# Samples' attention: float32 products on four strips of 32 array columns in place of two-part products per sequence, and a scan in two halves

## The chip, the cores and the metric

One core of one Trainium2 chip runs the whole kernel. The metric is the device time of one execution in microseconds; the kernel before has a median of 1036.18 us over three runs (1036.05 to 1041.79).

## What is computed

One step of a decoder layer for 512 prompt tokens and for 32 sample tokens: 8 sequences with 4 new tokens each and 1024 past tokens in pages of 128. Two attention branches read the same normalised input; a gated merge, an output projection, a SwiGLU FFN and a last norm follow. Everything is float32. The change concerns the two branches of the samples alone. Branch b (stick-breaking, 8 heads of 64) and branch a (softmax over 256 chosen keys, 8 query heads on 2 key heads) are, cut to what matters:

```python
# branch b, per sequence: q_b (4, 8, 64), keys and values (1028, 8, 64)
z = einsum('bthd,bshd->bhts', q_b, k) * HEAD_DIM ** -0.5
log_beta = log_sigmoid(z)
log_rest = where(strict, log_beta - z, 0.0)
later = cumsum(log_rest, axis=3, reverse=True) - log_rest
a = where(strict, exp(log_beta + later), 0.0)
o = einsum('bhts,bshd->bthd', a, v)
# branch a, per sequence: keys and values (1028, 2, 64), sel = the 256 chosen by the indexer
s = einsum('btcgd,btncd->btcgn', qg, sel_k) * HEAD_DIM ** -0.5
o = einsum('btcgn,btncd->btcgd', softmax(s), sel_v)
```

## The kernel before

A float32 matrix product is made of three or two products of fp32r operands: each operand is split into a part `h` (a copy rounded to fp32r, on ScalarE) and a rest `l` (the difference, on VectorE or POOL). Weights are split in `Weights._split` (L109 to L122), tokens once.

After the indexer's part (up to about 165 us), three generators are merged by `beside` (L1384): `samples` (budget S_COST), `heads` (the prompt's two attentions, H_COST) and the dense chain of projections and branch products (D_COST, matmuls at L504). `beside` always advances the stream whose share of yielded cost is lowest, so the yields and the budgets set how the streams mix; the tile framework's scheduler then orders the instructions of each engine once, when the program is built. On the chip each engine works through its queue in that order. The steps of top-k for the samples run beside (L639).

`samples` runs `sb_sample` (branch b) and then `dsa_sample` (branch a).

Branch b goes through two halves g of four sequences each. `logits` walks over two pairs of sequences, over c (pairs of pages), over b (the sequence of the pair) and jj (two pairs of heads each). `keys` (L1026) loads two pages of keys by `page` (SP's queue; at most eight page loads are outstanding, KV_B = 6 buffers of 128 x 512), turns them on TensorE (L1036, four transposes into one bank of tag `ts`), copies the bank rounded to `kk` on ScalarE (L1040) and takes the rest on VectorE (L1041). `scores` (L1055) multiplies, with queries of hi and lo parts in 128 stationary columns, four times per (c, b, jj) at L1063: 256 columns of keys each, 288 where the new tokens' keys stand behind. `sum_parts` (L1010) adds the hi and lo rows (ScalarE copy, VectorE add). `weights` (L1086) makes two sigmoids, one reversed scan over all 1056 keys (VectorE) and a product, yields W_LAT, turns the weights (L1100, L1104) and splits them. `values` (L1112) loads the value pages of one sequence after the other, splits each (ScalarE L1124, VectorE or POOL L1125) and multiplies with 64 stationary columns and 512 moving (L1131, two per page; the new tokens' values `vnew` have 32 rows). `fold` (L1144) turns the outputs (L1147) and adds the parts.

Branch a has its rows gathered by POOL (`keys_values`). Per pair of sequences `keys` (L1173) turns (L1177), copies (L1181) and takes the rest (L1182); `products` (L1188) adds the mask as a product (L1191) and four products of the parts (L1194); the softmax follows; `values` turns the weights (L1237), splits values (L1225 ScalarE, L1226 POOL), multiplies (L1249) and folds by a product with `stacked` (L1260).

`ones` and `sq` at L1518 and L1519, behind the samples' part, are plain float32 products on the whole array, and so are those of L817 in the indexer's part; transposes are float32 too.

## Time and profile before

| | us |
|---|---|
| median of three runs | 1036.18 |
| the profiled execution, its own time | 1040.26 |
| its span, first to last instruction | 1038.4 |
| PE busy / DVE / ACT / POOL | 978.4 / 772.9 / 548.5 / 400.8 |

PE is TensorE's matmuls, PEld its weight loads, DVE VectorE, ACT ScalarE, POOL GpSimd, SP the engine that issues most DMAs. In a group's row stand the line and engine, the operation, the tile written and those read (out<-in), the array's rows*columns and the shape, the count, then busy us and mean ns of one, and behind the last bar the idle time just before and what ended it. A matmul's length includes its way through the array, so successive matmuls overlap and their starts tell more than their lengths. In a matmul's shape 128*64 means 128 rows and 64 stationary columns, 128x512 the 512 moving columns.

### The profile page before, as it was taken

What the parts mean: (1) busy time and instruction counts of PE and PEld (TensorE: products, weight loads), DVE (VectorE), ACT (ScalarE), POOL (GpSimd) and SP (SyncE); (2) the same over time, 40 slices, a digit from 0 to 9 for tenths busy, and PEclk for the clock granted to TensorE, in tenths of its full rate; (3) what the DMA queues carried; (4) which work ended last, traced back from release to release, by engine and by line L of the source; (5) the groups of instructions that cost most, each with busy time, mean ns of one, the idle gap of its engine ahead of it and who ended that gap; (6) DMA issues with size and microseconds to landing.
All of it is one profiled execution on the core that took longest, in us unless ns stands there. A gap on an engine that the chain in (4) does not pass through costs nothing.

```text
span 1038.4 us, 20529 instructions
## 1 busy us (share of the span) xinstructions
PE 978.4 (94%) x7374; PEld 925.7 (89%) x7374; DVE 772.9 (74%) x1521; ACT 548.5 (53%) x1089; POOL 400.8 (39%) x345
## 2 busy tenths in 40 slices
PE   5999999898899998999899999989999999999995
PEld 4999998787778998889689999989999999999995
DVE  4568996789887895777785766896787787875774
ACT  6224435466654655766687745543444445542453
POOL 4545545103762126462726844511233223200331
PEclk9999999899999999999899999999999999999998
DMA  9775646787886659854523873502433331234312
GB/s 276 184 201 165 165 125 200 250 225 211 233 251 204 203 168 286 244 195 144 180 80 130 281 207 103 143 21 82 120 96 91 102 100 49 65 89 138 107 46 87
DMA packets 184703, 162.13 MB, mean 156 GB/s; under 512 B 13338, under 2 KB 148058, under 8 KB 183578
## 3 DMA queue, kind: packets, MB, share of 16 engines
q1 hardware_dynamic: 179434, 145.85, 48.4%
q0 software_dynamic: 1872, 10.75, 3.0%
q10 hardware_dynamic: 3296, 4.23, 1.4%
q8 instruction: 58, 0.95, 0.4%
q14 instruction: 43, 0.35, 0.1%
HBM read 133.37 MB, written 22.01 MB: 150 GB/s over the span
## 4 chain that ended last, share of the span: by engine, by line
PE 69%; DVE 11%; DMA 8%; issue 5%; ACT 2%; POOL 2%; SPq 2%; ACTq 1%; DVEq 0%; POOLq 0%
PE mm L504 14%; PE ffB L1630 8%; PE ffC L1630 5%; PE ffA L1630 5%; PE acc L504 5%; PE acc L1131 3%; PE acc L1715 3%; PE z L504 2%; PE ts L1036 2%; PE acc L1063 2%; PE dnB L1808 2%; POOL wl L119 2%; PE tp L865 2%; PE tp L878 2%; DMA kb<-in_cache_kv_b 1%
## 5 line engine op out<-in xcount | busy, mean ns | idle before, releaser
L119 POOL TENSOR_TENSOR wl<-wst,wh 128x512 fp32r<-128x512 f32 (+2 forms) x136 | 167.4, 1252 | 176.5 <-ACT wh L115 154.0
L504 PE MATMUL mm<-xh,wh 128*128 128x256 f32 (+2 forms) x480 | 145.6, 303 | 9.1 <-ACT xh L1324 3.8
L504 PE MATMUL mm<-xh,wl 128*128 128x256 f32 (+2 forms) x480 | 141.6, 295 | 1.8 <-POOL wl L119 1.8
L504 PE MATMUL mm<-xl,wh 128*128 128x256 f32 (+2 forms) x480 | 141.8, 295 | 0.0
L239 POOL TENSOR_TENSOR wl<-wst,wh 128x512 fp32r<-128x512 f32 (+1 forms) x48 | 68.1, 1439 | 174.5 <-ACT wh L236 158.2
L504 PEld LDWEIGHTS mm<-xh,wh 128*128 128x128 f32 (+1 forms) x480 | 93.0, 194 | 14.2 <-ACT xh L1324 4.0
L115 ACT ACTIVATE wh<-wst 128x1024 fp32r<-128x1024 f32 (+3 forms) x83 | 75.1, 906 | 51.1 <-PE z L1715 17.8
L236 ACT ACTIVATE wh<-ws 128x1024 fp32r<-128x1024 f32 (+1 forms) x55 | 54.8, 997 | 80.9 <-PE ffB L1630 30.7
L504 PEld LDWEIGHTS mm<-xh,wl 128*128 128x128 f32 (+1 forms) x480 | 93.2, 194 | 3.4 <-POOL wl L119 2.0
L504 PEld LDWEIGHTS mm<-xl,wh 128*128 128x128 f32 (+1 forms) x480 | 92.6, 193 | 1.9 <-issue 0.9
L241 DVE TENSOR_TENSOR wl<-ws,wh 128x1024 fp32r<-128x1024 f32 (+1 forms) x55 | 66.0, 1200 | 5.5 <-ACT wh L236 5.5
L1125 POOL TENSOR_TENSOR vv<-vb,vv 128x512 fp32r<-128x512 f32 x24 | 35.1, 1463 | 56.0 <-ACT vv L1124 54.2
L1063 PE MATMUL acc<-kk,qb 128*128 128x256 f32 (+1 forms) x256 | 54.6, 317 | 1.6 <-DVE kk L1041 1.3
L1041 DVE TENSOR_TENSOR kk<-ts,kk 128x512 fp32r<-128x512 f32 x64 | 43.4, 682 | 12.8 <-ACT kk L1040 12.4
L1040 ACT ACTIVATE kk<-ts 128x512 fp32r<-128x512 f32 x64 | 37.8, 598 | 24.1 <-PE ts L1036 18.0
L1124 ACT ACTIVATE vv<-vb 128x512 fp32r<-128x512 f32 x64 | 38.1, 625 | 19.5 <-PE acc L1131 15.6
L1036 PE MATMUL ts<-ident,kb 128*128 128x128 f32 x256 | 42.2, 287 | 5.4 <-DMA kb<-in_cache_kv_b 2.1
L1125 DVE TENSOR_TENSOR vv<-vb,vv 128x512 fp32r<-128x512 f32 x40 | 42.1, 1057 | 6.9 <-ACT vv L1124 6.8
L504 PE MATMUL acc<-xh,wl 128*128 128x288 f32 (+1 forms) x160 | 47.0, 295 | 0.0
L236 ACT ACTIVATE wh<-wst 128x1024 fp32r<-128x1024 f32 (+1 forms) x34 | 34.9, 1025 | 22.7 <-PE ffB L1630 14.5
L504 PE MATMUL acc<-xh,wh 128*128 128x288 f32 (+1 forms) x160 | 46.5, 294 | 0.0
L504 PE MATMUL acc<-xl,wh 128*128 128x256 f32 (+1 forms) x160 | 46.5, 292 | 0.0
(505 smaller groups left out, 3438.7 us busy)
## 6 DMA issues: line engine op xcount, KB each, us to landing
wst<-in_w_in SPq DMA_DIRECT2D x38, 512.0 KB, 4.7
kb<-in_cache_kv_b SPq DMA_DIRECT2D x64, 256.0 KB, 3.5
vb<-in_cache_kv_b SPq DMA_DIRECT2D x64, 256.0 KB, 3.9
wst<-in_w_ffn_gate SPq DMA_DIRECT2D x40, 256.0 KB, 3.1
wst<-in_w_ffn_up SPq DMA_DIRECT2D x40, 256.0 KB, 3.4
wst<-in_w_ffn_down SPq DMA_DIRECT2D x16, 320.0 KB, 3.2
gate_d<-rowy SPq DMA_DIRECT2D x16, 272.0 KB, 2.3
gt<-gate_d SPq DMA_DIRECT2D x16, 272.0 KB, 5.9
```

What stands on the lines that cost most here:

```text
L115: self.nc.scalar.activation(h, st, AF.Copy)
L119: self.nc.gpsimd.tensor_sub(l[:, k], st[:, k], h[:, k].bitcast(F32))
L236: self.nc.scalar.activation(h, src, AF.Copy)
L239: self.nc.gpsimd.tensor_sub(l[:, g], src[:, g], h[:, g].bitcast(F32))
L241: self.nc.vector.tensor_sub(l, src, h.bitcast(F32))
L504: nc.tensor.matmul(ps, ww[:, k, :m], aa[:, k, hs], start=(k == 0 and p == 0), stop=(k == nk - 1 and p == 2))
L1036: nc.tensor.transpose(tp[:, (2 * j + pg) * P:(2 * j + pg + 1) * P], V["kp"][pg][:, (2 * jj + j) * P:(2 * jj + j + 1) * P], ident)
L1041: nc.vector.tensor_sub(kk[:, 1, :, :2 * P], tpv, S(kk[:, 0, :, :2 * P]))
L1063: nc.tensor.matmul(z[:, :w], st, t[:, j, :w], start=(b + jj + j + v == 0), stop=(b + jj + j + v == 4))
L1124: nc.scalar.activation(vh, raw, AF.Copy)
L1125: (nc.vector if pg % 3 else nc.gpsimd).tensor_sub(vl, raw, S(vh))
L1630: nc.tensor.matmul(ps[:, g], ww[:, g, k, :], aa[:, k, :], start=(first and k == 0 and p == 0), stop=(k == 3 and p == 2), skip_group_check= ...
```

## The change

The samples' products use plain float32 operands, with no split. For four sequences at a time each one's queries (8 heads x 4 tokens = 32 columns) or weights stand in their own 32 columns of the array; keys and values move. `side_by_side` issues the four products, sequence 3 first, and asks the scheduler to keep them in program order. Their outputs are the four quarters of the partitions of one bank. So `logits` takes two pages of each of four sequences per step, `values` one page of each of four, and branch a likewise works on four sequences. Nothing is left to fold. The new tokens' keys have products of their own (`fresh`, 32 columns). Evictions go through `out_of`: two on ScalarE, one on VectorE, in turn. The page buffers are 12 (KV_B in the old pool, KV_C beside the branch), `kk` has 8 buffers of half the size. The keys are read from the upper half down, and sigmoid, scan and product run on keys 512 to 1055 first, then on 0 to 511 with the carried value; values are read from the last page to the first. W_LAT and LEAD are gone, S_COST is 130 in place of 200.

```diff
-S_COST = 200
...
-LEAD = 2
-W_LAT = 8
...
 KV_B = 6
-KH_B = 4
+KV_C = 6
+KH_B = 8
...
+    evict = cycle((nc.scalar, nc.scalar, nc.vector))
+    quarter = lambda n4: slice(n4 * 32, (n4 + 1) * 32)
+
+    def side_by_side(product):
+
+        for n4 in range(3, -1, -1):
+            ins = product(n4)
+            if n4 < 3:
+                tc.keep_in_program_order(ins)
+
+    def out_of(dst, ps):
+        eng = next(evict)
+        if eng is nc.scalar:
+            nc.scalar.activation(dst, ps, AF.Copy)
         else:
+            nc.vector.tensor_copy(dst, ps)
+
+    def turn_weights(dst, src, m=P):
+
+        n = src.shape[-1] // m
+        tp = lts()
+        for k in range(n):
+            nc.tensor.transpose(tp[:m, k * P:(k + 1) * P], src[:, k * m:(k + 1) * m], ident)
+        out_of(dst, tp[:m, :n * P].rearrange("p (k r) -> p k r", k=n))
...
-            kk = sp_.tile([P, 2, 2, 2 * P + NS], F32R, tag="kk", name="kk", bufs=KH_B)
-            nc.scalar.activation(kk[:, 0, :, :2 * P], tpv, AF.Copy)
-            nc.vector.tensor_sub(kk[:, 1, :, :2 * P], tpv, S(kk[:, 0, :, :2 * P]))
...
+            kk = sp_.tile([P, 2, 2 * P], F32, tag="kk", name="kk", bufs=KH_B)
+            out_of(kk, tp.rearrange("p (j k) -> p j k", j=2))
+            return kk
...
-                st = qb[:, b * 512 + (2 * jj + j) * P:b * 512 + (2 * jj + j + 1) * P]
-                for v, t in enumerate(kk):
-                    nc.tensor.matmul(z[:, :w], st, t[:, j, :w], start=(b + jj + j + v == 0), stop=(b + jj + j + v == 4))
-            if b + jj == 2:
-                sum_parts(sp_, zr[64 * (p % 2):64 * (p % 2) + 64, c * 2 * P:c * 2 * P + w], z, w)
+                side_by_side(lambda n4: nc.tensor.matmul(
+                    z[quarter(n4), :2 * P], qb[:, 4 * g + n4, 2 * jj + j, :], kks[n4][:, j, :],
+                    start=(jj + j == 0), stop=(jj + j == 2), skip_group_check=True))
...
+            def done(c, jj, kks):
+                if jj == 0:
+                    V["zs"] = acc()
+                scores(g, c, jj, kks, V["zs"])
+                if jj:
+                    out_of(zr[:, c * 2 * P:(c + 1) * 2 * P], V["zs"][:, :2 * P])
+
+            for c in cc:
+                raws = {}
+                for jj in range(2):
+                    kks = []
+                    for n4 in range(4):
+                        if jj == 0:
+                            raws[n4] = [rows_of_page(0, 4 * g + n4, pg) for pg in (2 * c, 2 * c + 1)]
+                        kks.append(keys(raws[n4], jj))
+                        yield 0.45
+                        if n4 == 1 and ahead:
+                            done(*ahead.pop())
+                            yield 1.2
+                    ahead.append((c, jj, kks))
+            done(*ahead.pop())
+            yield 1.2
+
...
-            r = sp_.tile([P, NKEY], F32, tag="sg", name="sbg", bufs=1)
-            nc.scalar.activation(r, zr, AF.Sigmoid, scale=-1.0)
-            nc.scalar.activation(zr, zr, AF.Sigmoid)
-            rr = r[:, ::-1]
-            nc.vector.tensor_tensor_scan(rr, rr, rr, 1.0, OP.mult, OP.bypass)
-            nc.gpsimd.tensor_mul(zr[:, :NKEY - 1], zr[:, :NKEY - 1], r[:, 1:])
-            yield W_LAT
...
+        def weights(half, zr, r, a):
+
+            lo, hi = (0, 512) if half == 0 else (512, NKEY)
+            nc.scalar.activation(r[:, lo:hi], zr[:, lo:hi], AF.Sigmoid, scale=-1.0)
+            nc.scalar.activation(zr[:, lo:hi], zr[:, lo:hi], AF.Sigmoid)
+            rr = r[:, lo:hi][:, ::-1]
+            nc.vector.tensor_tensor_scan(rr, rr, rr, 1.0 if half else r[:, hi:hi + 1], OP.mult, OP.bypass)
+            end = NKEY - 1 if half else hi
+            nc.vector.tensor_mul(zr[:, lo:end], zr[:, lo:end], r[:, lo + 1:end + 1])
+            if half:
+                turn_weights(a[:, 4:NPG], zr[:, 512:PAST])
+                turn_weights(a[:NS, NPG:], zr[:, PAST:], NS)
+
+        def values(g, zr, a):
+            o = acc()
+            for pg in range(NPG, -1, -1):
+                if pg == 4:
+                    turn_weights(a[:, :4], zr[:, :512])
+                raws = [rows_of_page(1, 4 * g + n4, pg) if pg < NPG else vnew.rearrange("p j c -> p (j c)") for n4 in range(4)]
+                m = P if pg < NPG else NS
+                side_by_side(lambda n4: nc.tensor.matmul(
+                    o[quarter(n4), :], a[:m, pg, quarter(n4)], raws[n4], start=(pg == NPG), stop=(pg == 0), skip_group_check=True))
+                yield 1.2
...
-                        vv = sp_.tile([P, 2, 512], F32R, tag="kk", name="vv2", bufs=KH_B)
-                        vh, vl = vv[:, 0], vv[:, 1]
-                        nc.scalar.activation(vh, raw, AF.Copy)
-                        (nc.vector if pg % 3 else nc.gpsimd).tensor_sub(vl, raw, S(vh))
-                        st, mv = a2[:, pg, n4].rearrange("p v c -> p (v c)"), (vh, vl)
-                    for v in range(2):
-                        nc.tensor.matmul(o[:64, :], st, mv[v], start=(pg + v == 0), stop=(pg + v == NPG + 1))
...
+        def products(g, cols, kts, sr, mx):
+
+            w = cols.stop - cols.start
             z = acc()
+            nc.tensor.matmul(z[:, :w], rowsel[:NS, g, :], mask_s[:, cols], start=True, stop=False, skip_group_check=True)
+            side_by_side(lambda n4: nc.tensor.matmul(
+                z[quarter(n4), :w], qad[:, 4 * g + n4].rearrange("p h t -> p (h t)"), kts[n4], start=False, stop=True,
+                skip_group_check=True))
+            nc.scalar.activation(sr[:, cols], z[:, :w], AF.Copy)
+            nc.vector.reduce_max(out=mx, in_=z[:, :w], axis=mybir.AxisListType.X)
+
...
+        def values(g, sr):
+            a = dp.tile([P, NPG + 1, P], F32, tag="pT", name="pT", bufs=1)
+            for half in range(2):
+                turn_weights(a[:, 4 * half:4 * half + 4], sr[:, half * 512:(half + 1) * 512])
+            turn_weights(a[:NS, NPG:], sr[:, PAST:], NS)
+            yield 4.0
             o = acc()
+            for j in range(NPG + 1):
+                m = P if j < NPG else NS
+                side_by_side(lambda n4: nc.tensor.matmul(
+                    o[quarter(n4), :P], a[:m, j, quarter(n4)], V["kav", 4 * g + n4][:, j, 1, :] if j < NPG else vanew,
+                    start=(j == 0), stop=(j == NPG), skip_group_check=True))
+                yield 0.35
+            if g == 0:
+                hold(2, V["kr"])
+                hold(3, dp)
+            ot = dp.tile([P, P], F32, tag="oa", name="oa", bufs=1)
+            out_of(ot, o[:, :P])
+            yield 1.5
             tp = lts()
+            nc.tensor.transpose(tp[:, :P], ot, ident)
+            ov = tp[:, :P].rearrange("p (n h t) -> p h n t", n=4, h=8)
             for c in range(2):
                 for e in range(2):
+                    dst = o_s[0][e * 64:e * 64 + 64, 2 * c:2 * c + 2, g * 16:(g + 1) * 16]
```

TensorE's queue, logits of branch b (kb is a key page, kk turned keys, qb queries, acc the bank of logits; x9 counts equal rows that follow each other). Before:

```order
L1036 MATMUL ts<-ident,kb 128x128 x4
L1063 MATMUL acc<-kk,qb 128x256 x9
L865 MATMUL tp<-ident,b 128x128 x3
L1036 MATMUL ts<-ident,kb 128x128 x4
L1063 MATMUL acc<-kk,qb 128x256 x4
L878 MATMUL tp<-pt,vs 128x256 x2
```

Now, with the buffers' numbers, since the rows differ by them alone:

```order
L1047 MATMUL ts_2354<-ident_70,kb_2213 128x128
L1055 MATMUL acc_2382<-kk_2318,qb_2060 32x256
L1055 MATMUL acc_2382<-kk_2276,qb_2060 32x256
L1055 MATMUL acc_2382<-kk_2229,qb_2060 32x256
L1055 MATMUL acc_2382<-kk_2185,qb_2060 32x256
L1055 MATMUL acc_2382<-kk_2318,qb_2060 32x256
L1055 MATMUL acc_2382<-kk_2276,qb_2060 32x256
L1055 MATMUL acc_2382<-kk_2229,qb_2060 32x256
L1055 MATMUL acc_2382<-kk_2185,qb_2060 32x256
L933 MATMUL z_2345<-kk_2100,qq_2099 128x128 x2
```

The products of four sequences stand behind each other, two rounds of four; before, products of one sequence stood behind its own four transposes.

TensorE's queue, values of branch b (vv is a split page, vb the page as loaded, a the weights). Before:

```order
L504 MATMUL mm<-xh,wh 128x288
L1131 MATMUL acc<-vv_4517,a_3640 64x512
L504 MATMUL mm<-xh,wl 128x288
L504 MATMUL mm<-xl,wh 128x288
L504 MATMUL mm<-xh,wh 128x288
L504 MATMUL mm<-xh,wl 128x288
L504 MATMUL mm<-xl,wh 128x288
L1131 MATMUL acc<-vv_4536,a_3640 64x512
```

Now:

```order
L501 MATMUL mm_4464<-xl_122,wh_3977 128x288
L1113 MATMUL acc_3618<-vb_4059,a2_2072 32x512
L1113 MATMUL acc_3618<-vb_4048,a2_2072 32x512
L1113 MATMUL acc_3618<-vb_4037,a2_2072 32x512
L1113 MATMUL acc_3618<-vb_4026,a2_2072 32x512
L856 MATMUL tp_4167<-ident_70,b_3892 128x128 x4
```

One product of a split page stood between the dense products; now the four sequences' pages, unsplit, stand together.

More of the change, by code (lines that the diff above doesn't have):

```diff
@@ new lines, in sb_sample, with rows_of_page @@
+        nc.gpsimd.memset(qb, 0.0)
+        for j in range(4):
+            for e in range(2):
+                r, h = slice(e * 64, e * 64 + 64), 2 * j + e
+                nc.vector.tensor_copy(qb[r, :, j, h * TS:(h + 1) * TS], qsm[r, j].rearrange("p (n t) -> p n t", n=NSEQ))
+        places = cycle([(V["kv"], KV_B)] * KV_B + [(sp_, KV_C)] * KV_C)
+        def rows_of_page(v, n, pg):
+            pool, bufs = next(places)
+            raw = pool.tile([P, 512], F32, tag="kv", name="kvb"[v:v + 1] + "b", bufs=bufs)
+            page(raw, kvb[:, :, v], n, pg, "o s h d -> s (o h d)")
+            return raw
@@ L1033, in keys @@
+        def keys(raws, jj):
             tp = lts()
@@ new lines, in fresh @@
+        def fresh(g, zr):
+            z = acc()
+            for j in range(4):
+                side_by_side(lambda n4: nc.tensor.matmul(
+                    z[quarter(n4), :NS], qb[:, 4 * g + n4, j, :], knew[:, j, :], start=(j == 0), stop=(j == 3), skip_group_check=True))
+            nc.vector.tensor_add(zr[:, PAST:], z[:, :NS], sbnew[:, g, :])
+        def weights(half, zr, r, a):
[9 more added lines that the diff above has]
+                turn_weights(a[:NS, NPG:], zr[:, PAST:], NS)
@@ L1145, in fold @@
             tp = lts()
             for j in range(4):
[L1147 to L1152 removed]
+                nc.tensor.transpose(tp[:, j * P:(j + 1) * P], ot[:, j, :], ident)
@@ L1154, in sb_sample @@
+            tpv = tp.rearrange("p (j n h t) -> p h j n t", j=4, n=4, h=8)
+            for j in range(4):
+                for e in range(2):
+                    r_ = slice(e * 64, e * 64 + 64)
+                    nc.vector.tensor_copy(o_s[1][r_, j, g * 16:(g + 1) * 16].rearrange("p (n t) -> p n t", n=4), tpv[r_, 2 * j + e, j])
+            yield 0.5
         for g in range(2):
             zr = sp_.tile([P, NKEY], F32, tag="zr", name="zr", bufs=1)
-            yield from logits(g, zr)
-            yield from weights(g, zr)
@@ L1158, in sb_sample @@
-            yield from values(g)
+            r = sp_.tile([P, NKEY], F32, tag="sg", name="sbg", bufs=1)
+            a = sp_.tile([P, NPG + 1, P], F32, tag="a2", name="a2", bufs=1)
+            fresh(g, zr)
+            yield 0.6
+            for half in (1, 0):
+                yield from logits(g, zr, (2 * half + 1, 2 * half))
+                weights(half, zr, r, a)
+                yield 1.0
+            yield from values(g, zr, a)
     def keys_values(pool, p):
@@ L1188, in products @@
-        def products(p, sr, mx, c, kh, kl):
-            w = 2 * P + (NS if c == 3 else 0)
-            z = acc()
-            nc.tensor.matmul(z[:, :w], rowsel[:NS, p, :], mask_s[:, c * 2 * P:c * 2 * P + w], start=True, stop=False)
-            for b in range(2):
-                for v, t in enumerate((kh, kl)):
-                    nc.tensor.matmul(z[:, :w], stat[p % 2][:, b, :], t[:, b, :w], start=False, stop=(b + v == 2))
-            sum_parts(dp, sr[:, c * 2 * P:c * 2 * P + w], z, w, mx[:, 4 + c:5 + c])
@@ new lines, in scores @@
+        def scores(g, sr, mx):
+            products(g, slice(PAST, NKEY), [kanew] * 4, sr, mx[:, 6:7])
+            yield 0.6
+            before = None
+            for half in range(2):
+                kts = []
+                for n4 in range(4):
+                    kts.append(keys(V["kav", 4 * g + n4], half))
+                    yield 0.45
+                    if n4 == 1 and before:
+                        products(g, slice(0, 512), before, sr, mx[:, 4:5])
+                        yield 1.4
+                before = kts
+            products(g, slice(512, PAST), before, sr, mx[:, 5:6])
+            yield 1.4
+            nc.vector.reduce_max(out=mx[:, 0:1], in_=mx[:, 4:7], axis=mybir.AxisListType.X)
@@ L1270, in dsa_sample, with hold @@
-        raws.append(keys_values(dp, 1))
-        yield G_LAT
-        for p in (0, 2):
-            yield from scores(p, raws[p])
-            yield from scores(p + 1, raws[p + 1])
-            for b in (p, p + 1):
-                yield from values(b, raws[b])
-                if p == 0:
-                    raws.append(keys_values(V["kr"] if b == 0 else dp, b + 2))
+        def hold(p, pool):
+            for b, raw in enumerate(keys_values(pool, p)):
+                V["kav", 2 * p + b] = raw
@@ L1281, in steps @@
+        for b, raw in enumerate(V["raws"][0]):
+            V["kav", b] = raw
+        hold(1, dp)
+        yield G_LAT
+        for g in range(2):
+            sr = dp.tile([P, NKEY], F32, tag="sr", name="sr", bufs=2)
+            mx = dp.tile([P, 8], F32, tag="mxs", name="mxs", bufs=2)
+            yield from scores(g, sr, mx)
+            yield from values(g, sr)
     def steps(gen, budget):
```

237 lines of the change are left out of this document (35 added, 202 removed).

## The prediction

> **What bounds the kernel now.** I read the page first, then busy time by stretch, then the groups by form in the stretch that the change touches, then TensorE's timeline for the step from one matmul to the next, and last what TensorE waits for.
>
> ```profile
> span 1038.4 us, 20529 instructions
> PE 978.4 (94%) x7374; PEld 925.7 (89%) x7374; DVE 772.9 (74%) x1521; ACT 548.5 (53%) x1089; POOL 400.8 (39%) x345
> ...
> GB/s 276 184 201 165 165 125 200 250 225 211 233 251 204 203 168 286 244 195 144 180 80 130 281 207 103 143 21 82 120 96 91 102 100 49 65 89 138 107 46 87
> ...
> PE 69%; DVE 11%; DMA 8%; issue 5%; ACT 2%; POOL 2%; SPq 2%; ACTq 1%; DVEq 0%; POOLq 0%
> ```
>
> TensorE is busy for 94% of the span and carries 69% of the chain that ended last. The changed work lies between 165 us (just before the first page of the samples' keys is turned) and 570 us (after their last fold):
>
> ```profile
> 165.00:463.00 298.00, 275.01 (x1952) 243.19 (x1952) 229.54 (x521) 182.80 (x387) 121.57 (x93) 0.95 0.76 224
> ...
> sum 405.00, PE 375.96 PEld 333.33 DVE 305.76 ACT 260.32 POOL 172.08; mean PE 187.98 PEld 166.66 DVE 152.88 ACT 130.16 POOL 86.04
> ```
>
> Columns: stretch, length, busy us (count) of PE, PEld, DVE, ACT and POOL, granted clock, DMA share, GB/s; the last row sums both stretches. TensorE has a matmul in flight in 376 of 405 us; VectorE stands at 75%, ScalarE at 64%. So TensorE bounds this part, and the change is worth first of all TensorE's time in it, then some of the 29 us without a matmul.
>
> **The products that go.** Four groups of matmuls on two-part (fp32r) operands are replaced:
>
> ```profile
> L1063 PE MATMUL acc<-kk,qb 128*128 128x256 f32 x192 | 40.6, 317 | 1.4 <-DVE kk L1041 1.3
> L1063 PE MATMUL acc<-kk,qb 128*128 128x288 f32 x64 | 14.1, 319 | 0.3 <-ACT kk L1040 0.3
> L1131 PE MATMUL acc<-vv,a 128*64 128x512 f32 x128 | 41.3, 411 | 4.5 <-DVE vv L1125 4.4
> L1131 PE MATMUL acc<-vnew,a 32*64 32x512 f32 x16 | 5.6, 419 | 0.0
> L1249 PE MATMUL acc<-va,pT 128*64 128x256 f32 x64 | 10.7, 303 | 0.0
> L1249 PE MATMUL acc<-vanew,pT 32*64 32x256 f32 x8 | 2.6, 326 | 0.0
> ```
>
> ```profile
> L1194 PE MATMUL acc<-kah,qap x32: 275/295/402, 469.7 to 544.3; 128*128 128x256 f32 x24, 128*128 128x288 f32 x8
> L1194 PE MATMUL acc<-kal,qap x32: 276/282/399, 470.0 to 544.4; 128*128 128x256 f32 x24, 128*128 128x288 f32 x8
> ```
>
> The second fence is the view of one line: duration least/median/most, first and last start, forms. Durations overlap, so I price a matmul by the step to the next start, from the timeline (start, length, what, count):
>
> ```profile
> 427.71 0.86 PE L1131 MATMUL acc<-vv,a 128*64 128x512 f32 x3
> 428.41 0.28 PE L504 MATMUL mm<-xh,wh 128*128 128x256 f32 x1
> 428.53 0.28 PE L504 MATMUL mm<-xh,wl 128*128 128x256 f32 x1
> ```
>
> Three of 512 columns step by 0.70 us, 0.233 each; 256 columns by 0.12, and 288 in proportion by 0.135. So L1063 takes 192 x 0.12 + 64 x 0.135 = 31.7 us, L1131 144 x 0.233 = 33.6, L1194 48 x 0.12 + 16 x 0.135 = 7.9 and L1249 72 x 0.12 = 8.6: together 81.8 us.
>
> **The products that come.** Each is now one float32 product with 32 stationary columns, four of them (one per sequence, on columns 96, 64, 32 and 0 of the array) behind each other in the queue: a quad. Per half of the samples there are 16 quads of 256 columns for the logits, 9 of 512 for the values, and in the sparse branch 2 of 512 and 9 of 128; for both halves 8192 + 9216 + 2048 + 2304 = 21760 columns of quads. Before has float32 products on the whole array:
>
> ```profile
> 657.99 0.62 PE L1518 MATMUL tp<-sqa,ones 128*128 128x272 f32 x2
> 658.44 0.62 PE L1519 MATMUL tp<-sq,ones 128*128 128x272 f32 x2
> 658.90 0.62 PE L1518 MATMUL tp<-sqa,ones 128*128 128x272 f32 x2
> ```
>
> Each is one matmul in the program and two records ("x2"): 0.455 us for 272 columns, 1.67 ns per column. No row of before uses a strip of the array, so whether four strips run beside each other is bounded from both sides. If they overlap entirely, a quad costs what one product costs: 21760 x 1.67 ns = 36.4 us. If not at all, four times that: 145.6 us. Between them lies another reading of the same rows: the second of a product's records needs the strip of the first and starts 0.23 us after it (half of 0.455); if starts keep the queue's order, the second record of one strip overlaps only the first of the next strip, and a quad takes two products' time: 72.8 us. I take the middle of the two readings in which strips overlap, 1.5 x 36.4 = 54.6 us (1.28 us for a quad of 512 columns). This side is nearer to the rows, since records that stand in the queue step by streaming time alone there, and nothing in them makes one strip wait for another's data.
>
> The Trainium skill (TensorE: Matmul & The Clock Gate, "Measured speedup vs the span model") reports a speedup of 3.07 for four row strips and 2.38 for three column strips. By 3.07 the quads would take 145.6/3.07 = 47.4 us and the forecast would be 7 us lower, an estimate from that page; no run here shows it.
>
> Gained on products: 81.8 - 54.6 = 27.2 us.
>
> **Smaller terms on TensorE.** The folds of the two parts go, and products get wider:
>
> ```profile
> L1260 PE MATMUL ts<-stacked,oa 64*128 64x32 f32 x32 | 4.3, 275 | 0.7 <-ACT oa L1255 0.7
> L1191 PE MATMUL acc<-mask_s,mb 32*128 32x256 bf16 x12 | 3.4, 287 | 0.0
> L1237 PE MATMUL ts<-ident,sr 64*128 64x64 f32 x32 | 3.2, 230 | 0.0
> L1147 PE MATMUL ts<-ident,ot 64*128 64x64 f32 x32 | 3.7, 235 | 0.0
> ```
>
> L1260's 4.3 us go. Of 16 mask products (0.28 us each) 4 of 512 columns and 2 of 32 stay, about 2 us less. Transposes of weights and outputs fall from 86 to 46; at 0.1 us (3.2/32, 3.7/32) that is 4 us. New are 40 products of 32 columns with the new tokens, 80 records: by columns 80 x 0.027 = 2 us, by the nearest row
>
> ```profile
> 125.98 1.00 PE L817 MATMUL tp<-qbi,kti 128*128 128x64 f32 x8
> ```
>
> (eight records in 1.00 us, with four times the stationary columns) 10 us. I take 5, since 32 columns stand nearer to the lower end. Net gain 5 us. The 320 transposes of keys stay.
>
> A change of the array's shape costs time where the trace has one:
>
> ```profile
> 269.64 0.19 PEld L1131 LDWEIGHTS acc<-vnew,a 32*64 32x64 f32 x2 [0.42 <-issue]
> ...
> 270.24 0.19 PEld L504 LDWEIGHTS mm<-xl,wh 128*128 128x128 f32 x1 [0.42 <-issue]
> ```
>
> Going into a 32-row product and out of it leaves the weight loader idle for 0.42 us each. The change visits column strips in some 45 places; before visits 32- or 64-row shapes in some 50, nearly all of which go. I put the difference at nothing, with 45 x 0.4 = 18 us of loss as its upper end. The skill (TensorEngine Tiling (Array Packing), "Key Properties") says that a change of mode drains the array; these rows agree for rows, and none shows columns.
>
> **Work taken from the other engines.**
>
> ```profile
> L1041 DVE TENSOR_TENSOR kk<-ts,kk 128x512 fp32r<-128x512 f32 x64 | 43.4, 682 | 12.8 <-ACT kk L1040 12.4
> L1125 DVE TENSOR_TENSOR vv<-vb,vv 128x512 fp32r<-128x512 f32 x40 | 42.1, 1057 | 6.9 <-ACT vv L1124 6.8
> L1182 DVE TENSOR_TENSOR kal<-ts,kah 128x512 fp32r<-128x512 f32 x16 | 10.8, 681 | 0.0
> L1125 POOL TENSOR_TENSOR vv<-vb,vv 128x512 fp32r<-128x512 f32 x24 | 35.1, 1463 | 56.0 <-ACT vv L1124 54.2 <-PE mm L504 1.8
> L1226 POOL TENSOR_TENSOR va<-kav,va 128x512 fp32r<-128x512 f32 x16 | 20.4, 1295 | 8.0 <-ACT va L1225 7.9
> L1124 ACT ACTIVATE vv<-vb 128x512 fp32r<-128x512 f32 x64 | 38.1, 625 | 19.5 <-PE acc L1131 15.6 <-PE acc L1063 2.0 <-DMA vb<-in_cache_kv_b 1.8
> L1225 ACT ACTIVATE va<-kav 128x512 fp32r<-128x512 f32 x16 | 9.6, 624 | 1.4 <-PE acc L1249 1.3
> ```
>
> The splits go: 96 us on VectorE, 55 on POOL, 48 on ScalarE. Evictions of transposes stay, and a third of them moves to VectorE (some 35 at 0.6 us, 21 us). All of it lies beside TensorE except where TensorE waited:
>
> ```profile
> L1036 PE MATMUL ts<-ident,kb 128*128 128x128 f32 x256 | 42.2, 287 | 5.4 <-DMA kb<-in_cache_kv_b 2.1 <-DVE kk L1041 1.7 <-issue 1.1
> L1063 PEld LDWEIGHTS acc<-kk,qb 128*128 128x128 f32 x256 | 38.6, 197 | 2.6 <-DVE kk L1041 1.6 <-ACT kk L1040 0.5 <-issue 0.3
> L1131 PEld LDWEIGHTS acc<-vv,a 128*64 128x64 f32 x128 | 16.2, 137 | 10.4 <-DVE vv L1125 6.2 <-ACT pt L868 0.4
> ```
>
> Behind the bar stands idle time and its cause. PE stood idle for 1.7 us before L1036 (DVE kk), and by the rows above for 1.3 before L1063 (DVE kk) and 4.4 before L1131 (DVE vv): 7.4 us, of which I credit 7. The weight loader's 1.6 and 6.2 are the same stalls or others; if others, 15 in all. The values now go from the DMA straight into the matmul and wait for the page instead. That side is bounded by two pieces of the chain:
>
> ```profile
> 184.65 5.82 DMA kb<-in_cache_kv_b
> ...
> 217.20 7.41 DMA kb<-in_cache_kv_b
> ```
>
> A quad needs the pages of four sequences at once (eight alive, before two); the buffers grow from 6 to 12. The same 128 loads stand in SP's one queue, among the loads of weights, which wait behind a page that has no buffer yet. If pages are late once more by what these pieces show, the term is -13 us instead of +7.
>
> The yield after the weights goes, and sigmoid, scan and product run in two halves. The upper half is hidden by the lower half's keys and the other streams' matmuls; without that cover it is about 4 us for each half of the samples.
>
> **Sum.** 27 + 5 + 7 = 39 us. The profiled execution took 1040.3 us for its span of 1038.4; the median of the runs shown is 1036.2. The gain is taken from the median: **997 us**.
>
> **Rivals.**
> *Full overlap.* Quads 36.4 us: 45.4 + 12 = 57 us gained, **979 us**. For it: strips share neither weights nor output partitions. Against it: the two records of one strip must follow each other.
> *Queue order.* Quads 72.8 us: 9 + 12 = 21 us gained, **1015 us**. For it: in every row of the timeline a start follows the start before it in the queue. The same page of the skill ("What overlaps and what doesn't") has matmuls start and end in program order; by that rule this case holds.
> *Pages bound.* The first stretch cannot shrink, and only the sparse branch's 16.5 - 10.9 us and the small terms, 11 us, are left: **1025 us**. For it: DMA share 0.76 at 224 GB/s, and the pieces of 5.82 and 7.41. Against it: losing 28 of 298 us asks for 247 GB/s, and the page's slices reach 286.
> *No overlap* (the change does not do what it is built for). Quads 145.6 us: 63.8 lost, 12 gained, **1088 us**, slower. Its place is every quad, and it decides from 93.8 us of quads on, 2.6 times one product, 2.2 us for a quad of 512 columns. For it: no row of before shows two matmuls on the array at once. Against it: each instruction names its own strip.
>
> **Chances.** Forecast 0.37, full overlap 0.20, queue order 0.20, pages 0.09, no overlap 0.14. A measurement of this kernel can tell about 1% (10 us) from no change. Faster by over 1%: 0.37 + 0.20 + 0.15 + 0.05 = 0.77, where the last two are the shares of queue order and pages that keep 10 us; within 1%: 0.05 + 0.04 = 0.09; slower: 0.14. The range goes from 968 (full overlap, 15 us of waits and a little more gone) to 1040 (queue order with late pages or drains); only the case without overlap lies outside. The forecast's own range is 978 to 1016: quads at 1.2 to 1.8 times one product (11 us either way) and part of the waits' bounds.
>
> **What would show it.** In the profile after, two quads of 512 columns that stand back to back lie 1.28 us apart (0.86 full overlap, 1.71 queue order, 3.4 none). VectorE falls by some 75 us over the samples' part, ScalarE by 60 to 70, POOL by 55. The first 165 us and everything behind the samples keep their length. I am wrong if a quad of 512 columns takes over 2.2 us, if pages ("DMA kb", "DMA vb") carry over 30 us of the chain, or if the part shortens without TensorE's work getting less.

## The result, and the profile after

The changed kernel takes 994.78 us (median of four runs, 991.3 to 997.11), the kernel before 1038.99 us (median of four). The ratio is 0.957, 95% interval 0.952 to 0.962: 44 us less. The forecast was 997 us, from the median of 1036.2 us that stood on record then.

The page of the kernel after; its lines answer to those that the prediction opened with:

```profile
span 995.3 us, 19970 instructions
PE 932.3 (94%) x7412; PEld 864.7 (87%) x7412; DVE 671.2 (67%) x1319; ACT 475.0 (48%) x949; POOL 332.2 (33%) x292
```

TensorE is busy for the same share of a shorter span: 46 us less busy time. Over the whole span VectorE lost 102 us, ScalarE 73, POOL 69. Busy time by stretch, cut where branch a's first keys are turned and behind the last fold (columns as in the prediction):

```profile
165.00:424.00 259.00, 232.39 (x1891) 184.97 (x1889) 153.25 (x394) 124.26 (x275) 70.09 (x58) 0.95 0.85 257
424.00:505.00 81.00, 77.87 (x715) 69.04 (x715) 46.08 (x137) 49.03 (x125) 24.83 (x26) 1.00 0.45 147
505.00:995.30 490.30, 471.35 (x3680) 465.32 (x3678) 352.36 (x516) 234.48 (x410) 157.05 (x128) 0.98 0.38 110
```

The samples' part now takes 340 us where it took 405. That is 65 us less, but what follows takes 490 us instead of 468 (1038.4 - 570): 22 us of dense work that used to lie beside the samples now stands behind them. A part that shrinks while other streams fill it gives back what it no longer covers. From the first FFN matmul to the end both kernels take nearly the same (360.5 and 358.9 us).

The groups that replaced the fp32r products:

```profile
L1055 PE MATMUL acc<-kk,qb 128*32 128x256 f32 x256 | 18.9, 416 | 2.1 <-DVE kk L1016 2.1
L1113 PE MATMUL acc<-vb,a 128*32 128x512 f32 x128 | 18.6, 621 | 3.2 <-DMA vb<-in_cache_kv_b 3.2
L1163 PE MATMUL acc<-kat,qad 128*32 128x512 f32 x32 | 4.3, 605 | 0.0
L1199 PE MATMUL acc<-kav,pT 128*32 128x128 f32 x128 | 3.9, 274 | 0.0
```

One visit to the column strips, in TensorE's timeline (start, length, what, count):

```profile
292.65 0.30 PE L501 MATMUL mm<-xl,wh 128*128 128x288 f32 x1
292.79 0.40 PE L933 MATMUL z<-kk,qq 128*128 128x512 f32 x1
293.11 1.07 PE L1113 MATMUL acc<-vb,a 128*32 128x512 f32 x8
294.11 0.49 PE L933 MATMUL z<-kk,qq 128*128 128x512 f32 x1
```

Eight records (four products of two) of 512 columns go in 1.00 us, from 293.11 to the next start at 294.11. One product of 512 columns alone costs 0.86 us by the prediction's price of 1.67 ns per column. So four products cost what one costs, and about 0.14 us to leave the strips; going in took 0.32 us where a matmul of 512 columns steps by 0.23, 0.09 us more. The eight records start in two bunches: four within 20 ns, the other four 0.45 us later. The change visits the strips 44 times. At the 35 visits that follow the dense chain, the heads or a transpose of keys, the step that leads in is longer than usual by 4 us in all; leaving costs some 6 us, an estimate (44 x 0.14) from this one visit.

To see where the time went, I summed the step from each matmul's start to the next start by kind of work, from 168 us to the first FFN matmul of bank B (684.0 us before, 642.5 after), without the time in which no matmul was in flight, which is counted apart. Dense chain means L504 (now L501), heads L865, L878, L942, L943 and L982 (now L856, L869, L933, L934 and L973); folds are those of L1260:

| steps of TensorE, us | before | after |
|---|---|---|
| samples' products (and folds, before) | 104.6 | 47.8 |
| dense chain, heads' matmuls | 321.3 | 330.9 |
| transposes of keys (branch b) | 26.5 | 32.2 |
| the rest | 35.0 | 30.5 |
| all steps | 487.4 | 441.3 |
| no matmul in flight | 28.5 | 32.9 |

The products fell by 57 us, their neighbours rose by 15, the waits by 4. Some 4 us of both are a matter of where a step is counted: before, the last transpose of keys ahead of a product stepped by 0.03 us and the first product behind it by 0.20 in place of 0.12; now the last transpose steps by 0.20 and what leaving costs is counted with the quads. The granted clock isn't lower than before; these windows, before and after, have the same:

```profile
168.00:684.00 516.00, 487.39 (x3562) 442.84 (x3563) 384.69 (x876) 323.91 (x677) 233.72 (x193) 0.97 0.65 195
168.00:642.50 474.50, 441.33 (x3601) 381.66 (x3601) 285.66 (x680) 251.69 (x539) 167.33 (x147) 0.97 0.70 212
```

What TensorE waits for now, the first rows of its list from 150 to 700 us:

```profile
PE mm L501 <- ACT rowy L546: 4.0, 2, 2.5
PE ts L1047 <- DMA kb<-in_cache_kv_b: 3.9, 6, 1.4
PE mm L501 <- ACT rowy L537: 3.7, 8, 1.1
PE acc L1113 <- DMA vb<-in_cache_kv_b: 3.2, 4, 2.1
```

(us in total, times, longest.) The splits are gone from this list, and pages stand in it instead.

### The profile page after: what moved, and what is told of

Same layout as the page of the kernel before. It is cut to its first block, busy times and chain, and to the rows that moved or that the text cites. A ratio compares the mean times of both kernels' runs of the same rounds, so it can differ in the third digit from the quotient of the medians.

```text
span 995.3 us, 19970 instructions
## 1 busy us (share of the span) xinstructions
PE 932.3 (94%) x7412; PEld 864.7 (87%) x7412; DVE 671.2 (67%) x1319; ACT 475.0 (48%) x949; POOL 332.2 (33%) x292
## 4 chain that ended last, share of the span: by engine, by line
PE 38%; DVE 6%; DMA 3%; issue 3%; ACT 2%; POOL 2%; SPq 0%; DVEq 0%; ACTq 0%; POOLq 0%
PE ffB L1582 9%; PE ffC L1582 5%; PE ffA L1582 5%; PE mm L501 3%; PE acc L1667 3%; PE dnB L1760 2%; PE z L1667 2%; POOL wl L117 2%; PE mm L1667 1%; PE dnC L1760 1%; PE acc L501 1%; DMA rowy<-od 1%; DVE wl L239 1%; PE z L501 1%; PE dnA L1760 1%
## 5 line engine op out<-in xcount | busy, mean ns | idle before, releaser
L117 POOL TENSOR_TENSOR wl<-wst,wh 128x512 fp32r<-128x512 f32 (+2 forms) x136 | 164.1, 1228 | 239.8 <-ACT wh L113 170.6
L501 PE MATMUL mm<-xh,wh 128*128 128x256 f32 (+2 forms) x480 | 148.6, 310 | 13.6 <-ACT rowy L546 4.0
L501 PE MATMUL mm<-xh,wl 128*128 128x256 f32 (+2 forms) x480 | 142.9, 298 | 2.4 <-POOL wl L117 2.4
L501 PE MATMUL mm<-xl,wh 128*128 128x256 f32 (+2 forms) x480 | 143.3, 298 | 0.0
L501 PEld LDWEIGHTS mm<-xh,wh 128*128 128x128 f32 (+1 forms) x480 | 94.0, 196 | 24.1 <-ACT rowy L537 5.3
L501 PEld LDWEIGHTS mm<-xh,wl 128*128 128x128 f32 (+1 forms) x480 | 93.8, 196 | 4.3 <-POOL wl L117 2.6
L501 PEld LDWEIGHTS mm<-xl,wh 128*128 128x128 f32 (+1 forms) x480 | 93.6, 195 | 2.0 <-issue 1.7
L501 PE MATMUL acc<-xh,wl 128*128 128x256 f32 (+1 forms) x160 | 46.1, 291 | 0.0
L501 PE MATMUL acc<-xl,wh 128*128 128x256 f32 (+1 forms) x160 | 45.8, 289 | 0.0
L501 PE MATMUL acc<-xh,wh 128*128 128x288 f32 (+1 forms) x160 | 45.5, 289 | 0.0
L237 POOL TENSOR_TENSOR wl<-raw,wh 128x384 fp32r<-128x384 f32 x14 | 14.2, 1038 | 80.2 <-ACT wh L234 64.2
L860 DVE TENSOR_TENSOR pt<-tp,pt 128x128 fp32r<-128x128 f32 (+1 forms) x64 | 31.1, 487 | 13.6 <-ACT pt L859 13.3
L859 ACT ACTIVATE pt<-tp 128x128 fp32r<-128x128 f32 (+1 forms) x64 | 27.6, 433 | 25.4 <-PE tp L856 25.0
L1047 PEld LDWEIGHTS ts<-ident,kb 128*128 128x128 f32 x256 | 29.8, 145 | 10.6 <-DMA kb<-in_cache_kv_b 3.3
L537 ACT ACTIVATE rowy<-mm 128x256 f32<-128x256 f32 (+1 forms) x40 | 15.8, 395 | 48.1 <-PE mm L501 37.7
L563 POOL TENSOR_TENSOR rowl<-rowy,rowh 128x512 fp32r<-128x512 f32 (+1 forms) x18 | 23.2, 1288 | 38.0 <-DVE rowh L561 16.2
```

The costliest lines, as they stand in the source:

```text
L117: self.nc.gpsimd.tensor_sub(l[:, k], st[:, k], h[:, k].bitcast(F32))
L237: self.nc.gpsimd.tensor_sub(l[:, g], src[:, g], h[:, g].bitcast(F32))
L501: nc.tensor.matmul(ps, ww[:, k, :m], aa[:, k, hs], start=(k == 0 and p == 0), stop=(k == nk - 1 and p == 2))
L859: nc.scalar.activation(hi, tpv, AF.Copy)
L860: nc.vector.tensor_sub(lo, tpv, S(hi))
L1047: nc.tensor.transpose(tp[:, (2 * j + pg) * P:(2 * j + pg + 1) * P], raws[pg][:, (2 * jj + j) * P:(2 * jj + j + 1) * P], ident)
```

## The experiments

The theory after the result (**TensorE's time**): four strips overlap entirely, the quads' shorter time on TensorE is the gain, a part of it goes back in changes of the array's shape and in waits. The rivals: **relief** (the gain comes from splits that no longer hold up pages, banks and queues), **mix** (it comes from the other budget, which orders the streams differently), and **pages** (transfers bound what is left). All times are medians; the change has 994.8, before 1037.7 to 1039.1 beside each set.

**one_strip.** Do strips overlap, and does it matter?

```diff
-                    o[quarter(n4), :P], a[:m, j, quarter(n4)], V["kav", 4 * g + n4][:, j, 1, :] if j < NPG else vanew,
+                    o[:32, n4 * P:(n4 + 1) * P], a[:m, j, quarter(n4)], V["kav", 4 * g + n4][:, j, 1, :] if j < NPG else vanew,
...
-            out_of(ot, o[:, :P])
+            for n4 in range(4):
+                out_of(ot[quarter(n4), :], o[:32, n4 * P:(n4 + 1) * P])
```

> Branch a's values (36 products of 128 columns per half, each two records) all stand on array columns 0 to 31, their four outputs beside each other in one bank; nothing is left out. In the change a half's 36 products took 2.24 us from the first start to the next other matmul. If strips run beside each other and that is what the change gains, a half takes 36 x 0.213 = 7.7 us here and the whole time rises by about 11 us, to 1006. If products of one strip overlap as well (or the strips never mattered), the length stays near 2.2 us and the time within 2 us of the change.

Measured: 1007.6 us, 12.8 more than the change. (In this arrangement branch a doesn't give the layer's sums, though its expectation says that nothing is left out; only its time is read.) The timeline of one half, of one_strip:

```profile
457.20 7.17 PE L1199 MATMUL acc<-kav,pT 128*32 128x128 f32 x64
464.31 1.06 PE L1199 MATMUL acc<-vanew,pT 32*32 32x128 f32 x8
465.30 0.18 PE L1162 MATMUL acc<-mask_s,mb 32*128 32x32 bf16 x1
```

and of the change:

```profile
456.65 1.95 PE L1199 MATMUL acc<-kav,pT 128*32 128x128 f32 x64
458.54 0.42 PE L1199 MATMUL acc<-vanew,pT 32*32 32x128 f32 x8
458.89 0.18 PE L1162 MATMUL acc<-mask_s,mb 32*128 32x32 bf16 x1
```

The 32 products of the pages take 7.11 us on one strip and 1.89 on four, 3.8 times less. Both halves together: 2 x (8.10 - 2.24) = 11.7 us more on TensorE and 12.8 us in the whole. The strips do overlap, and TensorE's time counts one for one.

**strip_major.** Must the strips alternate in the queue?

```diff
-            for j in range(2):
-                side_by_side(lambda n4: nc.tensor.matmul(
+            for n4 in range(3, -1, -1):
+                for j in range(2):
+                    ins = nc.tensor.matmul(
...
```

> Logits alone: both products of strip 3 (four records) stand ahead of both of strip 2, and so on, where the change has one product of each strip and then the second of each. If TensorE looks past records that wait for their own strip, a visit of 16 records stays at 1.0 us and the time at that of the change (995). If starts follow the queue, each strip's four records start one after the other, 0.21 us apart, ahead of the next strip's: about 3 us for a visit, 16 visits, 30 us more: 1025. A window of fewer records than four gives something between, 1.5 to 2 us for a visit and 8 to 16 us more.

Measured: 997.0 us. The timeline of strip_major:

```profile
213.08 1.09 PE L1056 MATMUL acc<-kk,qb 128*32 128x256 f32 x16
214.10 0.39 PE L501 MATMUL mm<-xh,wh 128*128 128x256 f32 x1
```

Sixteen records in 1.02 us, 1.00 in the change. In the built program the queue has the strips at columns 96, 96, 64, 64, 32, 32, 0, 0, so four records for one strip stand ahead of the next strip's first. The records start in four bunches of four, 0.04 us within a bunch and some 0.22 from bunch to bunch. The trace doesn't name a record's strip; but records of one strip start 0.11 us apart for 128 columns in one_strip (64 in 7.11 us), so 0.22 for 256. So a bunch is one record of each strip, and the other strips don't wait for the first. Starts don't keep the queue's order across strips, so "each engine works through its queue in that order", as the text ahead of the prediction has it, needs that exception.

**doubled.** TensorE's time alone is put back, with the other engines relieved as in the change.

```diff
+                for again in range(2):
+                    side_by_side(lambda n4: nc.tensor.matmul(
...
```

(in the logits and likewise in the values of branch b)

> The change with every quad of branch b issued twice in a row, so that its sums are doubled (which changes the outputs of branch b) and nothing but TensorE gets more work: 32 quads of 256 columns and 18 of 512, 32 x 0.43 + 18 x 0.86 = 29 us. If TensorE's time is what counts beside waits, the whole takes 25 to 33 us longer, 1020 to 1028, with the other engines' work as in the change. If TensorE's time is hidden behind pages and evictions there, under 12 us more: under 1007.

Measured: 1027.3 us, 32.5 more. Two quads of 512 columns back to back, in the timeline of doubled:

```profile
254.92 1.93 PE L1115 MATMUL acc<-vb,a 128*32 128x512 f32 x16
256.78 0.33 PE L933 MATMUL z<-kk,qq 128*128 128x128 f32 x1
```

They take 1.86 us, so the second adds 0.86, one product's time. The visits together take 34 us more (some quads were scheduled apart, which adds visits), and the whole took 32.5 us more. In branch b too, TensorE's time counts one for one.

**splits_back** and **splits_apart.** The other engines' work alone is put back; TensorE's stays short.

```diff
+            if v:
+                hi, lo = idle_parts()
+                nc.scalar.activation(hi, raw, AF.Copy)
+                (nc.vector if pg % 3 else nc.gpsimd).tensor_sub(lo, raw, S(hi))
...
+            _, lo = idle_parts()
+            nc.vector.tensor_sub(lo.rearrange("p (j k) -> p j k", j=2), tp.rearrange("p (j k) -> p j k", j=2), kk)
```

> The change with the old splits put back as idle work that no matmul reads: each value page is copied on ScalarE and subtracted on VectorE or POOL, each bank of turned keys is subtracted on VectorE, as before (about 48 us of ScalarE, 96 of VectorE, 35 of POOL); one page buffer fewer (5 for KV_C) makes the room. If the change gains on TensorE's products, the time rises by under 10 us (under 1005), by buffers and banks that come free later. If it gains by relieving the other engines, most of the 44 us comes back: 1025 or more.

> As splits_back, but the idle copies and differences go to several scratch buffers (two and three, bf16), so that one idle piece doesn't wait for the one before it; KV_C is 4 (the run buf4 has that alone). If the 76 us of splits_back came from its single scratch buffers, this stands within 15 us of buf4. If the work itself costs (it holds pages and banks longer and stands ahead of other work in the queues of VectorE, ScalarE and POOL), most stays: 30 us or more above buf4.

Measured: splits_back 1071.2 us, splits_apart 1023.3, against 989.9 of its control buf4. Of the 81 us by which splits_back stands above buf4, 48 went with its single scratch buffers (and with the bf16 type of the copies and one page buffer less, which were changed with them); that run tells nothing about relief. The other 33 us stay; by the expectation that is the case in which the work itself costs. Groups of splits_apart:

```profile
L1060 DVE TENSOR_TENSOR il<-ts,kk 128x512 bf16<-128x512 f32 x64 | 42.6, 683 | 8.6 <-ACT kk L1014 8.2
L1042 ACT ACTIVATE ih<-vb 128x512 bf16<-128x512 f32 x64 | 39.4, 627 | 24.1 <-DVE il L1043 14.2 <-POOL il L1043 5.0 <-DMA vb<-in_cache_kv_b 2.9
L1055 PE MATMUL ts<-ident,kb 128*128 128x128 f32 x256 | 39.1, 282 | 8.3 <-DVE il L1060 4.0 <-ACT sk L576 2.2 <-DMA kb<-in_cache_kv_b 1.0
```

No matmul reads `il`, yet the transposes of keys wait 4.0 us for it, because it holds their bank, and ScalarE stands idle for 24.1 us ahead of the copies, 19.2 of them until `il` has read an earlier copy. Idle time of TensorE over the table's stretch is 51.8 us (buf4 33.5), and its steps are 451.5 us (433.7) for the same matmuls, at a granted clock of 0.97 (0.99). So relief is worth up to 33 us where TensorE's products are short (up to, since the scratch buffers still hold ScalarE). Before, the same splits left TensorE only 28.5 us idle in all, 7.4 of them by the splits as the prediction read it; that its own longer products covered the rest is argued, since no run takes the splits alone out of the kernel before.

**buf4** and **half_values.** Do pages bound what is left?

```diff
-KV_C = 6
+KV_C = 4
```

```diff
-                raws = [rows_of_page(1, 4 * g + n4, pg) if pg < NPG else vnew.rearrange("p j c -> p (j c)") for n4 in range(4)]
+                if pg % 2 or pg == NPG:
+                    raws = [rows_of_page(1, 4 * g + n4, pg) if pg < NPG else vnew.rearrange("p j c -> p (j c)") for n4 in range(4)]
```

> The change with 10 page buffers in place of 12 (KV_C 4), so two pages beyond the eight that a step of the keys needs. If pages that come late are what is left of the waits (7.1 us of idle time by the trace of the change), fewer buffers make them later: 3 to 10 us more, 998 to 1005. If the buffers are ample, within 2 us of the change.

> Leaves out half of the value pages' loads (even pages are multiplied with the rows of the odd ones), so that 32 of 128 page loads, 8 MB, are gone and nothing else. If the change is still bound by TensorE, only the waits for value pages (3.2 us) and the lower clock after them go: 988 to 993. If transfers bound branch b (DMA share 0.85 at 257 GB/s there), 8 MB at that rate are 31 us, and 15 to 30 us go: 965 to 980.

Measured: buf4 989.9 us (ratio to before 0.956, interval 0.948 to 0.963, which cannot be told from the change's 0.957; neither expected range, 998 to 1005 or within 2 us of 994.8, has it), though TensorE's waits for value pages rose from 3.2 to 6.7 us. Two buffers fewer cost nothing that shows. half_values took 986.8 us (0.950, interval 0.944 to 0.956): 8 us less than the change, a little beyond the 988 to 993 expected of a part bound by TensorE and far from the 15 to 30 us of a part that transfers bound. Value pages cause waits; they are not the bound. Pages of keys were all still loaded in this run.

**b_only** and **a_only.** One branch changed at a time. Both are the kernel before with one branch's functions from the change and a budget by the sum of the yields:

```diff
-S_COST = 200
+S_COST = 150
...
-                    nc.tensor.matmul(z[:, :w], st, t[:, j, :w], start=(b + jj + j + v == 0), stop=(b + jj + j + v == 4))
+                side_by_side(lambda n4: nc.tensor.matmul(
```

```diff
-S_COST = 200
+S_COST = 178
...
-    qad = wk.tile([P, 8, NS], F32, name="qad")
+    qad = wk.tile([P, NSEQ, 8, TS], F32, name="qad")
```

> Branch b as in the change, branch a as before (budget of the samples 150, by the sum of the yields). If the gain follows TensorE's time in the products (before: 31.7 + 33.6 us at branch b, 7.9 + 8.6 + 4.3 at branch a), branch b carries three quarters: 33 of 44 us, time 1006. If it follows the splits on the other engines, branch b has five sixths: 1002, which this run does not tell from it. If pages bound branch b, it carries half or less: 1015 or more.

> Branch a as in the change, branch b as before (budget 178 by the sum of the yields). TensorE's steps in branch a's products fall by 17 us from before to the change by the traces, so by TensorE's time alone: 1022. If the parts of the change work only together (b_only gained nothing: its 40 us of shorter products were lost to 22 us more idle time and a lower clock), it takes more or less than that: above 1030, or below 1010.

Measured: b_only 1042.3 us (ratio 1.003, interval 1.001 to 1.005), a_only 1032.1 (0.994, interval 0.991 to 0.997). Alone, at these budgets, they bring -3 and 7 us, together 44. a_only's number is its second case, parts that work only together. The third case of b_only's expectation, pages as the bound, would fit its number, but half_values speaks against it, and so does the next run, which loads the same pages. The steps of branch b's products were as short in b_only as in the change (17.2 and 21.7 us for logits and values with the new tokens'; 18.9 and 20.2 in the change), so the products did not fail. TensorE's timeline of b_only, with idle time before a matmul in brackets:

```profile
402.56 1.94 PE L1132 MATMUL acc<-vb,a 128*32 128x512 f32 x8 [6.61 <-DMA vb<-in_cache_kv_b]
405.52 1.93 PE L1132 MATMUL acc<-vb,a 128*32 128x512 f32 x8 [1.02 <-DMA vb<-in_cache_kv_b]
408.57 1.93 PE L1132 MATMUL acc<-vb,a 128*32 128x512 f32 x8 [1.12 <-DMA vb<-in_cache_kv_b]
...
425.42 1.01 PE L981 MATMUL z<-kaa,qqa 128*128 128x384 f32 x2 [7.00 <-DVE mx L984]
```

The values stand there with little else beside them; TensorE waits for pages, and then runs slowly: eight records of a quad take 1.93 us that take 1.07 elsewhere. The stretch in b_only has a granted clock of 0.62:

```profile
400.00:430.00 30.00, 17.91 (x85) 12.04 (x86) 12.50 (x30) 6.67 (x15) 8.05 (x7) 0.62 0.71 226
```

**b_only125** and **before165.** Is it the mix?

```diff
-S_COST = 150
+S_COST = 125
```

```diff
-S_COST = 200
+S_COST = 165
```

> b_only with the samples' budget at 125 in place of 150: the samples are advanced earlier or later against the dense chain and the heads, and nothing else changes. If b_only gained nothing because its mix leaves waits (6.6 us for a value page at 402 us, 7.0 for VectorE at 425, 3.8 for a load at 378), another mix moves these and the time by 10 us or more, towards 1010 to 1030. If the shorter products of branch b are worth nothing by themselves, it stays within 8 us of 1042.

> The kernel before with the samples' budget at 165 in place of 200 and nothing else: against the sum of the samples' yields (about 172 us there, 119 in the change) that is 0.96, as b_only125 has 0.95, while before has 1.16 and the change 1.09. If a good part of the change's 44 us is the mix that its budget gives, as 31 us were in b_only, the kernel before gains 10 us or more as well: 1029 or less. If the products carry the gain and b_only was badly mixed only with new branch b beside old branch a, it stays within 8 us of 1039.

Measured: b_only125 1010.9 us (0.975, interval 0.970 to 0.980): one number took 31 us off b_only. The same stretch in b_only125:

```profile
400.00:430.00 30.00, 24.36 (x183) 19.21 (x183) 16.17 (x43) 12.83 (x31) 11.38 (x11) 0.99 0.87 269
```

TensorE ran 183 matmuls there instead of 85, at a clock of 0.99. Idle time over the table's stretch fell from 50.9 to 32.0 us and steps from 470.9 to 458.2. So branch b alone brings 28 us once the other streams are placed to cover it. before165 took 1047.8 us (1.009, interval 1.006 to 1.012): the kernel before gains nothing from this smaller budget, it loses 10 us. That speaks against the change's 44 us being a better mix of the same work; other budgets of the kernel before, and of a_only, were not tried.

**merged.**

```diff
-KV_C = 6
-KH_B = 8
+KV_C = 4
+KH_B = 10
...
+                for jj in range(2):
+                    scores(g, c, jj, both[jj], z)
...
```

> The logits' four quads of one pair of pages stand together (8 visits to the column strips of four quads in place of 16 of two), with 10 buffers of kk and 10 page buffers (KV_C 4 as in buf4, 989.9). A visit costs about 0.2 us beyond its quads by the trace of the change (0.08 going in, 0.13 coming out): 8 fewer are 2 us, which a measurement can't tell; the trace should show 1.87 us for a visit of four quads in place of 2 x 1.0. Where keys are late because 10 tiles of turned keys are alive, it is slower than buf4 by 3 us or more.

Measured: 1000.3 us, 10 more than buf4. It doesn't test what it was made for: in its trace the scheduler issued the quads by two again (16 records) in 15 of 17 visits, and idle time before the transposes of keys rose from 6.9 us (buf4) to 9.6. What a visit costs is known from the timeline alone, not from a run with fewer visits.

## Why the prediction was right, step by step

- **The bound.** Right: TensorE's time counts nearly one for one, 32.5 us for 34 (doubled) and 12.8 for 11.7 (one_strip).
- **The products that come: 54.6 us forecast; mis-sized.** "I take the middle of the two readings": the reading with full overlap (36.4 us) holds. A quad costs 0.86 us for 512 columns where the forecast had 1.28. All visits together take 47.8 us, with leaving the strips, the new tokens' small products and stretches of low clock. The middle was a compromise between two mechanisms of which one was wrong. The rival queue order doesn't hold across strips: by strip_major a start passes records that wait for another strip. The rule of the Trainium skill (TensorE: Matmul & The Clock Gate, "What overlaps and what doesn't") that was named with it, matmuls in program order without reordering, doesn't hold across strips here either.
- **The products that go: 81.8 us forecast, too low.** Start to start they and the folds took 104.6 us (forecast 81.8 + 4.3). Steps in the middle of a run (0.12, 0.233) were read rightly. Of the 19 us that the products took beyond them, some 6 stand in the last step of each run, some 4 in stretches of low clock and the rest inside the runs, about half of it in the first step (0.20 us at L1063 with 256 columns). On products and folds together 57 us went where the forecast had 27.2 + 4.3 - 5, about 26.
- **The smaller terms: 5 us forecast.** The masks took 2.2 us less (about 2 forecast) and the small transposes 2.9 (4 forecast). The new tokens' 40 products cost about 1.4 us by their steps, below the lower of the two prices that the prediction gave (2 and 10) and below the 5 taken.
- **Changes of the array's shape: nothing forecast, with 18 us as the upper end.** The steps of the neighbours rose by 15 us (table). Some 4 of them are what going into the strips adds and some 4 the border of the count (the 0.03 us steps of before); what leaving costs stands in the quads' 47.8. Lower clock is none of it: the neighbours' steps at a granted clock under 0.9 stand about 10 us above the usual step in both traces. Another 4 or 5 us stand in steps that end in a wait, where the last matmul runs out before TensorE stands idle; the remaining 3 have no cause that was found. Going in and leaving together come to some 10 us by these estimates, between the two values of the prediction; what the visits of before cost isn't told apart from their products.
- **Waits: 7 us of gain forecast, 4.4 of loss measured.** The splits' waits went as forecast; waits for pages and evictions took their place (28.5 to 32.9 us in all). It lies within the bound of -13 us that the prediction gave, but the sign of the term was wrong.
- **"All of it lies beside TensorE except where TensorE waited."** This holds only while TensorE is as slow as before. With short products the same splits cost up to 33 us (splits_apart against buf4). The sum was not hurt, because the change takes both away at once; whoever had kept the splits would have met them. So the two parts don't add up: short products with the splits kept stand 16 us below the kernel before (splits_apart, 1023.3 against 1038.8), the relief with 34 of the products' 57 us put back 12 us below it (doubled, 1027.3 against 1039.1), both together 44.
- **The scan in two halves.** The weights' transposes wait 0.8 us for it in the trace after, against the 4 us for each half of the samples without cover. No run undid it by itself.
- **The marks.** Quads of 512 columns lie 0.86 us apart (doubled), the mark of full overlap. TensorE's waits for pages sum to 7.1 us; the chain of the trace after reaches back only to 445.8 us, behind branch b, so the pages' share of it can't be read. Both kernels' first 165 us keep TensorE busy for the same time (150.7 us). VectorE fell by 102 us against 75 forecast: the adds of `sum_parts` (16 x 0.42 and 32 x 0.25 us, L1015 and L1017) and the copies of the new tokens' keys (4.7 us, L1043), 19 us together, were left out. ScalarE fell by 73 (60 to 70 forecast), POOL by 69 (55).

So 997 against 994.8 is luck: two errors cancel, 30 us too little for the products against 11 us for waits and 15 us at the products' neighbours that were not charged. The mechanism, TensorE's shorter products, is right; the size of no large term is.

## What to carry to other kernels

Products that use a quarter of the array's columns can be set four side by side for the time of one, and plain float32 then costs less than two-part operands (47.8 us here against 104.6). Work on other engines is credited only with the waits it causes today, but its price changes once the bound engine gets faster; ask what it would cost then, and take it away in the same step. After a stream has become shorter, set its share of the mix anew and measure it: with the same products a budget of 125 instead of 150 was worth 31 us in b_only, while a smaller budget cost the kernel before 10.

## What the runs showed of the hardware

**A wait can cost twice.** Behind some waits of a few microseconds TensorE ran on at a lower granted clock. In the kernel after:

```profile
277.10 0.61 PE L501 MATMUL mm<-xh,wh 128*128 128x288 f32 x1 [2.54 <-ACT rowy L546]
277.51 0.45 PE L501 MATMUL mm<-xh,wl 128*128 128x288 f32 x1
277.75 0.45 PE L501 MATMUL mm<-xl,wh 128*128 128x288 f32 x1
277.99 0.45 PE L501 MATMUL mm<-xh,wh 128*128 128x288 f32 x1
```

```profile
276.00:278.00 2.00, 0.90 (x4) 0.90 (x5) 1.48 (x5) 1.43 (x5) 0.00 (x0) 0.69 0.69 187
278.00:281.00 3.00, 3.00 (x17) 3.00 (x17) 1.18 (x3) 0.00 (x0) 1.90 (x1) 0.64 0.59 178
```

Behind a wait of 2.54 us the dense products step by 0.24 us; in the timeline above, at 292.65, one steps by 0.14. The granted clock is 0.69 and 0.64 in these two windows, and 0.50 from 276.8 to 280.2 us. Not every wait does this: behind one of 2.06 us, in the same kernel, the clock stayed at 1.00.

```profile
342.66 1.07 PE L1055 MATMUL acc<-kk,qb 128*32 128x256 f32 x16 [2.06 <-DVE kk L1016]
342.70:346.00 3.30, 3.30 (x33) 2.72 (x34) 3.30 (x5) 1.71 (x3) 0.00 (x0) 1.00 0.80 239
```

What starts and ends such a stretch was not tested.

**Strips run on by themselves.** The second record of a product starts 0.45 us behind the first for 512 columns, while records behind it in the queue have already started on other strips (read from the bunches of four in the timelines of the change and of strip_major).
